# Making the sums of up-projection weight blocks during the input projection instead of in the first feed-forward block

## The chip, the cores and the metric

The kernel runs on one core of one Trainium2 chip. A core has a matmul engine (TensorE, PE in the profile, with its weight loads as PEld), a vector engine (VectorE, DVE), an activation engine (ScalarE, ACT), a general engine (GpSimd, POOL) and a queue engine (SyncE, SP) that only issues transfers. ACT and POOL issue transfers too. The metric is the device time of one execution, in microseconds (us); lower is better.

## The reference

One layer of a hybrid encoder is computed for two groups of requests that share the weights: one prompt of 2048 rows (16 tiles of 128) and 8 short sequences of 16 rows (one tile, the sample).

```python
def layer(x, ...):
    h = rms_norm(x, norm_g[0])
    z = h @ w_in                      # 1024 -> 3592: q, k, v of 8 attention heads; q, k, v, o and gates of 4 mLSTM heads
    att = rms_norm(band_attention(qa, ka, va, rel_table), g_att)   # own chunk of 64 and 8 chunks before
    hb = mlstm_sequence(qh, kh, vh, ig, lf, c0, n0, m0)            # matrix memory, running maximum
    x = x + rms_norm(concat([att, gated(hb)]) @ w_out, norm_g[1])
    x = x + rms_norm(conv_ffn(rms_norm(x, norm_g[2]), ...), norm_g[3])

def conv_ffn(h, buf, w_up, w_conv, b_conv, w_down):
    u = h @ w_up                      # 1024 -> 2 x 2816
    y = b_conv + sum(ext[:, j:j + S] * w_conv[j] for j in range(3))   # causal depthwise convolution
    gate, up = jnp.split(y, 2, axis=-1)
    return (gelu(gate) * up) @ w_down
```

What the change touches is `h @ w_up`, and there only when and where some sums of weight blocks are made.

## The kernel before

All products are made in a split form: each operand is divided into a rounded high part and the rest, and `mm3` (L103) issues three matmuls, high by high, high by low and low by high (L105, L106, L107 in the profile). The division of an operand is one ACT copy and one VectorE subtraction (`split`, L1323; the rows of L1324 and L1325).

The program has three parts.

**The input projection** (the loop at L1260). The 3592 columns are cut into 14 groups, and the rows into two halves, so there are 28 turns (`seq`). In a turn `group_rows` or `group_T` multiplies one group's weights with the half's rows and yields after every 12 matmuls; each yield is one step of the loop at L1288. In each step the next group's weights are loaded and divided bit by bit (`load_group`), and `pump` (L184) advances two software pipelines beside the projection: attention (`att_stream`, for the sample `attention_sample`) and the mLSTM (`mem_stream`), as long as a running account of estimated VectorE time stays behind a share of estimated TensorE time. Loads go through SP, stores of the projection through ACT.

**The output projection** (`project`, L970). Beside it `folds` (L1172) forms combinations of blocks of `w_down` in six spare tiles of 128 x 512 (`spare_tile`, L70): loads and stores on POOL's queue, subtractions on VectorE (L1184), each pinned behind what was written before it on its engine by `keep_in_program_order`. At its end `h2_units` builds the seven combinations B of the feed-forward input for the first block; four of them pass through DRAM (`lated`) and are divided later (`late_B`, L1163).

**The feed-forward network** (the loop at L1478) runs over three blocks of rows. The up-projection uses a seven-product scheme on 2 x 2 blocks: for each of 22 feature tiles the four stored blocks a11, a12, a22, a21 of `w_up` (128 x 512 each) and four sums of them

- s1 = a21 + a22, s2 = s1 - a11, s3 = a11 - a21, s4 = a12 - s2

give the weights of seven products: a11, s2, s3, s1 in the first group of a feature tile and a12, a22, s4 in the second. `load_quads` (L1329) brings them in, `load_up` (L1356) divides them. In the first block (`b == 0`) `load_quads` loads the four stored blocks through SP, makes the four sums on VectorE (L1341), stores them through POOL to a DRAM tensor `wsd` (L1343), and keeps three tiles for the second group. In the second and third block the sums are read from `wsd` through SP (L1352), seven loads for each feature tile. All these tiles come from a pool of eleven (`quad`, L1063).

A program that plans ahead orders each engine's instructions by a model of their durations; only pinned ones keep their written place behind the instruction before them. [...] A tile of a pool is written again only when those who read it before have signalled.

Of the kernel before, what the change touches and what calls it, by code (L numbers as in the profile page):

```python
# [13 lines left out]
ALU = mybir.AluOpType  # L14
# [14 lines left out]
NF = 22  # L29
# [21 lines left out]
def hymba_step(ctx: ExitStack, tc: tile.TileContext, I: dict, O: dict):  # L51
    nc = tc.nc
# [17 lines left out]
    def spare_tile(name):  # L70
        return spare.tile([P, 512], F32, tag="k", name=name)

    def dt_(shape, name):
        return dram.tile(shape, F32, tag=name, name=name)
# [52 lines left out]
    wsd = [dt_([P, 2048], f"wsd{f}") for f in range(NF)]  # L127
# [143 lines left out]
    def group_rows(wh, wl, half, chunks, dst, name, width=256, out=None):  # L271
        for ci, tiles in enumerate(HALVES[half]):
            for j, t in enumerate(tiles):
                ch = chunks[ci]
                acc = ps_mm(f"{name}_{t}")
                for k in range(KT):
                    w = slice(k * width, (k + 1) * width)
                    tt = slice(j * P, (j + 1) * P)
                    mm3(acc[:, :width], ch[:, 0, k, tt], ch[:, 1, k, tt], wh[:, w], wl[:, w],
                        start=(k == 0), stop=(k == KT - 1))  # L280
                    if k % 4 == 3:
                        yield 1.3, 0.0
                stage = pa.tile([P, 384], F32, tag="st", name=f"{name}_st{t}", bufs=2)
                evac_scaled(stage[:, :256], acc[:, :256], None)
                if width > 256:
                    nc.vector.tensor_copy(gates[:, gate_ix(t), :], acc[:, 256:width])
                s = 4 if t == SAMPLE else t // 4
                nc.scalar.dma_start(dst[s][:, 0 if s == 4 else t % 4, :], stage[:, :256])
                if out is not None and s >= 3:
                    nc.scalar.dma_start(out[s - 3][:, 0 if s == 4 else t % 4, :], stage[:, :256])  # L290
# [4 lines left out]
    def raw_tile(name):  # L295
        return pa.tile([P, LS], F32, tag="raw", name=name, bufs=3)
# [3 lines left out]
    def load_bias():  # L300
        rel.append(raw_tile("reln")[:HA, :SQ - 383])
        tc.keep_in_program_order(nc.sync.dma_start(rel[0], I["rel_rev"][:, 0:SQ - 383]))
# [528 lines left out]
    def prep(units):  # L831
        yield units
        yield FLUSH
# [229 lines left out]
    def quad(name):  # L1063
        return ffn.p3.tile([P, 512], F32, tag="q", name=name, bufs=11)
# [107 lines left out]
    def folds():  # L1172
# [17 lines left out]
        for k in range(NK + 1):  # L1190
# [19 lines left out]
            make(k, 1, 2, 1, sub)  # L1210
            yield

    GROUPS = ["va0", "qk0", "qk1", "va1", "qk2", "qk3", "qb0", "vo0", "qb1", "vo1", "qb2", "vo2", "qb3", "vo3"]
    SRC = {g: i for i, g in enumerate(["va0", "qk0", "qk1", "va1", "qk2", "qk3",
                                       "qb0", "vo0", "qb1", "vo1", "qb2", "vo2", "qb3", "vo3"])}

    def load_group(gi):

        i = SRC[GROUPS[gi]]
        src, n = (I["w_in0"], 2112) if i == 0 else (I["w_in1"][i - 1], 2048)  # L1220
        h = wpool.tile([P, 2112], F32R, tag="wh", name=f"wi{i}_h{gi}", bufs=2)
        l = wpool.tile([P, 2112], F32R, tag="wl", name=f"wi{i}_l{gi}", bufs=2)

        def steps():
            q = n // 2
            for s in range(2):
                raw = pr.tile([P, 1056], F32, tag="wraw", name=f"wi{i}_raw{s}")
                nc.sync.dma_start(raw[:, :q], src[:, s * q:(s + 1) * q])
                yield 0.0, 0.0
                yield 0.0, 0.0  # L1230
                for e in range(2):
                    c = slice(s * q + e * q // 2, s * q + (e + 1) * q // 2)
                    r = raw[:, e * q // 2:(e + 1) * q // 2]
                    nc.scalar.copy(h[:, c], r)
                    nc.vector.tensor_tensor(l[:, c], r, h[:, c], op=ALU.subtract)
                    yield 0.0, 0.6

        return h, l, steps()
# [18 lines left out]
        pass  # L1257
    next(norms)
    load_bias()
    for n_, (half, gi) in enumerate(seq):  # L1260
        wh, wl, _ = pend
        split = iter([])
        if n_ + 1 < len(seq):
            pend = load_group(seq[n_ + 1][1])
            split = pend[2]
        g = GROUPS[gi]
        i = int(g[2])
        nm = f"{g}_{half}"
        if g[:2] == "va":
            it = group_rows(wh, wl, half, chunks, vd[i], nm, 264 if gi == 0 else 256,  # L1270
                            [O["v_prompt"][i], O["v_sample"][i].unsqueeze(1)])
        elif g[:2] == "qk":
            it = group_T(wh, wl, half, chunks, [qTd[i], kTd[i]], [-(DA ** -0.5), None], nm,
                         [None, [O["k_prompt"][i], O["k_sample"][i]]])
        elif g[:2] == "qb":
            it = group_T(wh, wl, half, chunks, [[t_[:, c, :] for t_ in qkbd[i]] for c in range(2)],
                         [None, DH ** -0.5], nm)
        else:
            it = group_rows(wh, wl, half, chunks, vobd[i], nm)
        if half == 0 and gi == 13:  # L1280
            chunks = []
            norms = norm_steps(1)
        if n_ == len(seq) - 1:
            out = project([0, 1, 2, 3, 4, 5, 6, 7, SAMPLE, 8, 9, 10, 11, 12, 13, 14, 15])
            split = w_out_steps()
            next(split)
            next(out)
        for u, (pe, dve) in enumerate(it):  # L1288
            ahead = []
            if n_ < len(seq) - 1 or u >= 6:  # L1290
                ahead.append(next(split, (0.0, 0.0)))
            if n_ == len(seq) - 1 and u == 12:
                ahead.append(next(out))
            if (half == 0 and gi == 13 and u >= 6 and u % 2 == 0) or (gi == 0 and u % 2 == 0):
                ahead.append(next(norms, (0.0, 0.0)))
            pump(pe + sum(a[0] for a in ahead), dve + sum(a[1] for a in ahead))
        for _ in split:
            pass
        if gi == 0:
            if half == 0:  # L1300
                nc.sync.dma_start(bgate, I["b_gate"].broadcast_to([P, 8]))
                nc.sync.dma_start(gatt, I["g_att"])
                heads.append(build_bias)
                mems.append(lambda: prep(prep_sample()))
            mems.append(lambda half=half: prep(prep_prompt(half)))
        if g[:2] == "qk":
            attention(i, half)
            if half == 0 and i == 3:
                heads.insert(len(heads) % 4, lambda: attention_sample(0, EARLY))
            if half == 1 and i == 0:  # L1310
                heads.insert(len(heads) % 4, lambda: attention_sample(EARLY, DB))
        if g[:2] == "vo":
            mems.append(lambda i=i, half=half: mlstm(i, half))
            if half == 0:
                mems.append(lambda i=i: mlstm_sample(i))
    for cost in out:
        pump(*cost)
    nc.sync.dma_start(O["m_prompt"], mrow[:, 16, :])
# [5 lines left out]
        nc.scalar.copy(h, r)  # L1324
        nc.vector.tensor_tensor(l, r, h, op=ALU.subtract)  # L1325

    raws = {}

    def load_quads(b, f, g):  # L1329

        src = lambda i: I["w_up"][f][:, i * 512:(i + 1) * 512]
        if b == 0 and g == 0:
            q = []
            for i in range(4):
                q.append(quad(f"wu{f}_{i}"))
                nc.sync.dma_start(q[i], src(i))
            a11, a12, a22, a21 = q
            s1, s2, s3, s4 = [quad(f"ws{f}_{i}") for i in range(4)]
            for o, x, y, op in ((s1, a21, a22, ALU.add), (s2, s1, a11, ALU.subtract), (s3, a11, a21, ALU.subtract),
                                (s4, a12, s2, ALU.subtract)):  # L1340
                nc.vector.tensor_tensor(o, x, y, op=op)  # L1341
            for i, o in enumerate((s2, s3, s1, s4)):
                nc.gpsimd.dma_start(wsd[f][:, i * 512:(i + 1) * 512], o)  # L1343
            raws[f] = [a12, a22, s4]
            return [a11, s2, s3, s1]
        if b == 0:
            return raws.pop(f)
        kept = lambda i: wsd[f][:, i * 512:(i + 1) * 512]
        out = []
        for i, s_ in enumerate([[src(0), kept(0), kept(1), kept(2)], [src(1), src(2), kept(3)]][g]):  # L1350
            r = quad(f"wu{b}_{f}_{g}_{i}")
            nc.sync.dma_start(r, s_)  # L1352
            out.append(r)
        return out
# [123 lines left out]
    for b, tiles in enumerate(FBLOCKS):  # L1478
# [48 lines left out]
        g, parts = {}, {}  # L1527
# [155 lines left out]
        if fast:  # L1683
# [96 lines left out]
            for p, (_, _, set_, onto) in enumerate(SEQUENCE):  # L1780
                for c in range(3):
# [19 lines left out]
                    for k in range(4 * c, min(4 * c + 4, NK)):  # L1801
                        i = 6 * p + k // 2
# [193 lines left out]
```

## Time and profile before

| | us |
|---|---|
| median of 3 runs | 2758.59 |
| lowest and highest run | 2757.4, 2761.65 |
| the profiled execution: its own time | 2761.56 |
| the profiled execution: its span | 2759.8 |

The granted clock of TensorE over the profiled execution is 0.988 of full speed. In the trace the input projection reaches to about 1022 us, the output projection from 1023 to 1327 us, the first block's up-projection from 1327 to 1668 us and its down-projection to about 1840 us; the second block follows to about 2330 us and the third to the end.

A row of grouped instructions reads: line, engine, operation, output <- inputs, count, then durations in ns. A row of waits reads: the engine and line that waited, whom it waited for, us in total, how many times, the longest. A row of a stage reads: from:to and its length, then the busy time of PE, PEld, DVE, ACT and POOL with counts of instructions, the granted clock, the share of the 16 DMA engines and GB/s. In order of time a row begins with its start and its duration, and ends in brackets with the idle time of the engine before it and what ended it.

### The profile page before, as it was taken

Reading aid. Unit: us, or ns where it says so; the run is one execution under the profiler, and the core shown is the slowest. Engines: PE = TensorE matmul, PEld = TensorE weight load, DVE = VectorE, ACT = ScalarE, POOL = GpSimd, SP = SyncE. Lnnn points to the kernel's source line nnn. Section 1 sums busy time; section 2 is a strip of 40 time slices with the busy share of each in tenths; the row PEclk is TensorE's granted clock in tenths of the full one; section 3 lists DMA queues with packets and bytes.
Section 4 is the critical chain, followed back from the end, with each engine's and each line's share of the span. In section 5 each row is a group of like instructions: output and inputs, shape, how many; then the busy total and the mean of one; then the engine's idle time right before and its main releaser. Section 6 shows DMA issues by size and latency. Waiting matters only on the chain.

```text
span 2759.8 us, 47655 instructions
## 1 busy us (share of the span) xinstructions
PE 2659.9 (96%) x16459; PEld 2481.2 (90%) x16459; DVE 1862.4 (67%) x3536; ACT 1417.6 (51%) x2887; POOL 700.7 (25%) x1325
## 2 busy tenths in 40 slices
PE   8899999999999999979899999999999999999998
PEld 7899999999799998867799998889999878999976
DVE  5345445644355666556898998758888776899956
ACT  4345544533355665433454456655454665555554
POOL 1100000211000002344655542023333212466401
PEclk9999999999999999989999999999999999999999
DMA  5634454556743554469877768766786777788775
GB/s 173 171 114 138 122 186 140 172 176 196 225 135 116 157 178 146 146 228 308 298 246 215 214 198 265 251 208 195 223 219 192 228 252 238 213 246 237 253 257 183
DMA packets 333711, 555.70 MB, mean 201 GB/s; under 512 B 61762, under 2 KB 169374, under 8 KB 333150
## 3 DMA queue, kind: packets, MB, share of 16 engines
q1 hardware_dynamic: 250798, 405.03, 47.5%
q0 software_dynamic: 44080, 113.81, 14.1%
q10 hardware_dynamic: 38592, 33.83, 3.7%
q8 instruction: 129, 2.11, 0.3%
q14 instruction: 112, 0.92, 0.1%
HBM read 389.77 MB, written 172.18 MB: 204 GB/s over the span
## 4 chain that ended last, share of the span: by engine, by line
PE 41%; DMA 5%; DVE 4%; issue 2%; ACT 1%; POOL 0%; DVEq 0%; SPq 0%; POOLq 0%; ACTq 0%
PE uec L105 5%; PE uec L106 5%; PE uec L107 5%; PE dn L107 3%; PE dn L105 3%; PE dn L106 3%; PE ua L107 3%; PE ua L106 3%; PE ua L105 3%; DMA wu<-in_w_up 2%; PE dnm L107 1%; PE dnm L106 1%; PE dnm L105 1%; PE ub L107 1%; PE ub L106 1%
## 5 line engine op out<-in xcount | busy, mean ns | idle before, releaser
L105 PE MATMUL uec<-B,wuh 128*128 128x384 f32 (+1 forms) x720 | 236.6, 329 | 9.2 <-DVE ug L1495 5.9
L106 PE MATMUL uec<-B,wuh 128*128 128x384 f32 (+1 forms) x720 | 235.4, 327 | 0.0
L107 PE MATMUL uec<-B,wul 128*128 128x384 f32 (+1 forms) x720 | 234.3, 327 | 0.0
L1324 ACT CAST wuh<-wu 128x512 fp32r<-128x512 f32 x255 | 141.6, 618 | 102.6 <-PE uec L106 98.7
L107 PE MATMUL dn<-wdh,al 128*128 128x512 f32 x462 | 186.0, 403 | 3.4 <-DVE al L1325 3.4
L105 PE MATMUL dn<-wdh,ah 128*128 128x512 f32 x462 | 183.6, 397 | 5.9 <-ACT ah L1324 4.0
L1325 DVE TENSOR_TENSOR al<-ar,ah 128x768 fp32r<-128x768 f32 (+2 forms) x141 | 108.4, 779 | 118.4 <-ACT ah L1324 114.8
L106 PE MATMUL dn<-wdl,ah 128*128 128x512 f32 x462 | 182.8, 396 | 0.0
L1324 ACT CAST ah<-ar 128x768 fp32r<-128x768 f32 (+2 forms) x141 | 96.2, 692 | 153.2 <-PE dnm L106 113.9
L1325 DVE TENSOR_TENSOR wul<-wu,wuh 128x512 fp32r<-128x512 f32 x255 | 164.3, 682 | 2.4 <-ACT wuh L1324 2.4
L663 POOL TENSOR_SCALAR ad<-ad 128x2 f32<-128x2 f32 x32 | 6.3, 195 | 615.3 <-DVE ad L661 615.3
L410 DVE CUSTOM_DVE_ANT_0 tmp<-s,nb 128x640 f32<-128x640 f32 (+4 forms) x128 | 94.1, 737 | 100.1 <-PE s L400 99.5
L105 PE MATMUL vo<-wi_h,hT 128*128 128x256 f32 x544 | 155.5, 286 | 0.0
L107 PE MATMUL vo<-wi_h,hT 128*128 128x256 f32 x544 | 155.3, 285 | 0.0
L106 PE MATMUL vo<-wi_l,hT 128*128 128x256 f32 x544 | 154.9, 285 | 0.0
L1325 DVE TENSOR_TENSOR wdl<-wdr,wdh 128x512 fp32r<-128x512 f32 x231 | 145.3, 684 | 8.2 <-ACT wdh L1324 8.0
L105 PEld LDWEIGHTS uec<-B,wuh 128*128 128x128 f32 x720 | 135.2, 188 | 13.6 <-issue 6.8
L105 PE MATMUL qk<-hT,wi_h 128*128 128x384 f32 (+1 forms) x384 | 130.3, 339 | 9.9 <-ACT qk_st L239 6.2
L411 ACT ACTIVATE tmp<-tmp,mn 128x640 f32<-128x640 f32 (+4 forms) x128 | 97.7, 763 | 77.0 <-DVE mn L410 72.6
L106 PEld LDWEIGHTS uec<-B,wuh 128*128 128x128 f32 x720 | 135.4, 188 | 0.2
L107 PEld LDWEIGHTS uec<-B,wul 128*128 128x128 f32 x720 | 135.1, 188 | 0.0
L1324 ACT CAST wdh<-wdr 128x512 fp32r<-128x512 f32 x231 | 127.4, 619 | 11.8 <-PE uec L106 7.4
(473 smaller groups left out, 9101.8 us busy)
## 6 DMA issues: line engine op xcount, KB each, us to landing
wu<-in_w_up SPq DMA_DIRECT2D x220, 256.0 KB, 4.8
wu<-wsd SPq DMA_DIRECT2D x176, 256.0 KB, 4.7
wdr<-wtd SPq DMA_DIRECT2D x132, 256.0 KB, 5.1
wi_raw<-in_w_in SPq DMA_DIRECT2D x52, 512.0 KB, 4.2
wdr<-in_w_down SPq DMA_DIRECT2D x99, 256.0 KB, 4.7
wsd<-ws POOLq DMA_DIRECT2D x88, 256.0 KB, 4.8
ar<-ad_S SPq DMA_DIRECT2D x50, 384.0 KB, 4.0
kraw<-kTd SPq DMA_DIRECT2D x112, 128.0 KB, 3.1
```

What stands on the lines that cost most here:

```text
L105: nc.tensor.matmul(out, ah, bh, start=start, stop=False, skip_group_check=onto)
L106: nc.tensor.matmul(out, ah, bl, start=False, stop=False, skip_group_check=onto)
L107: nc.tensor.matmul(out, al, bh, start=False, stop=stop, skip_group_check=onto)
L410: nc.vector.tensor_tensor_reduce(o_, s_, b_, 1.0, 3e38, ALU.add, ALU.min, accum_out=mn)
L411: nc.scalar.activation(tmp[:, :n], tmp[:, :n], AF.Exp, bias=mn, scale=-1.0, accum_out=rsum[:, i % 4, hh:hh + 1])
L663: nc.gpsimd.tensor_scalar(ad, ad, 1.0 / DH, 0.0, op0=ALU.mult, op1=ALU.add)
L1324: nc.scalar.copy(h, r)
L1325: nc.vector.tensor_tensor(l, r, h, op=ALU.subtract)
```

## The change

The sums are made by a new generator, `up_sums`, in the six spare tiles. It is advanced once in every step of the input projection from the third turn on (`n_ >= 2`), and whatever is left of it is run before the output projection's loop. For each feature tile it loads the four stored blocks through SP (two, a step, two), passes eight steps, makes the four sums on VectorE in four steps (three of them in place: s3 over a21, s2 over a11, s4 over a12), and stores them through POOL to `wsd` in two steps. Loads, sums and stores are pinned. `load_quads` loses its special case: the first block reads its seven weights as the two others do. The scheme's sums and the layout of `wsd` are as before. The short description of the change also speaks of sample attention in four column positions and of masks in DRAM; the kernel before has both, and the diff does not touch them.

```diff
+    def up_sums():
+
+        keep = tc.keep_in_program_order
+        for f in range(NF):
+            a11, a12, a22, a21 = q = [spare_tile(f"up{f}_{i}") for i in range(4)]
+            for i in range(4):
+                keep(nc.sync.dma_start(q[i], I["w_up"][f][:, i * 512:(i + 1) * 512]))
+                if i == 1:
+                    yield
+            for _ in range(8):
+                yield
+            s1 = spare_tile(f"up{f}_s")
+            for o, x, y, op in ((s1, a21, a22, ALU.add), (a21, a11, a21, ALU.subtract), (a11, s1, a11, ALU.subtract),
+                                (a12, a12, a11, ALU.subtract)):
+                keep(nc.vector.tensor_tensor(o, x, y, op=op))
+                yield
+            for i, o in enumerate((a11, a21, s1, a12)):
+                keep(nc.gpsimd.dma_start(wsd[f][:, i * 512:(i + 1) * 512], o))
+                if i % 2:
+                    yield
+
...
     load_bias()
+    sums = up_sums()
     for n_, (half, gi) in enumerate(seq):
...
         for u, (pe, dve) in enumerate(it):
             ahead = []
+            if n_ >= 2:
+                next(sums, None)
...
+    for _ in sums:
+        pass
     for cost in out:
         pump(*cost)
...
-    raws = {}
-
     def load_quads(b, f, g):
 
         src = lambda i: I["w_up"][f][:, i * 512:(i + 1) * 512]
-        if b == 0 and g == 0:
-            q = []
-            for i in range(4):
-                q.append(quad(f"wu{f}_{i}"))
-                nc.sync.dma_start(q[i], src(i))
-            a11, a12, a22, a21 = q
-            s1, s2, s3, s4 = [quad(f"ws{f}_{i}") for i in range(4)]
-            for o, x, y, op in ((s1, a21, a22, ALU.add), (s2, s1, a11, ALU.subtract), (s3, a11, a21, ALU.subtract),
-                                (s4, a12, s2, ALU.subtract)):
-                nc.vector.tensor_tensor(o, x, y, op=op)
-            for i, o in enumerate((s2, s3, s1, s4)):
-                nc.gpsimd.dma_start(wsd[f][:, i * 512:(i + 1) * 512], o)
-            raws[f] = [a12, a22, s4]
-            return [a11, s2, s3, s1]
-        if b == 0:
-            return raws.pop(f)
         kept = lambda i: wsd[f][:, i * 512:(i + 1) * 512]
```

## The prediction

> **What bounds the kernel now.** I read the page first, then busy time by stage, then who waited for whom in the stages that the diff touches.
>
> ```profile
> span 2759.8 us, 47655 instructions
> PE 2659.9 (96%) x16459; PEld 2481.2 (90%) x16459; DVE 1862.4 (67%) x3536; ACT 1417.6 (51%) x2887; POOL 700.7 (25%) x1325
> ```
>
> TensorE sets the end: it is busy for 2659.9 of 2759.8 us, so an edit can save at most the time in which TensorE idles or runs below its pace. Three stages by busy time: the stretch of the input projection in which the new sums would run, the up-projection of the first feed-forward block, and that of the second.
>
> ```profile
> core 0: us, PE busy (x) PEld busy (x) DVE busy (x) ACT busy (x) POOL busy (x), PEclk, DMA share, GB/s
> 80.00:928.00 848.00, 825.52 (x6267) 801.12 (x6266) 405.54 (x1014) 406.46 (x990) 52.86 (x160) 0.99 0.52 156
> 1326.70:1666.00 339.30, 326.97 (x1827) 318.92 (x1826) 315.99 (x488) 169.04 (x268) 182.40 (x271) 0.99 0.73 229
> 1843.00:2165.00 322.00, 321.47 (x1837) 319.96 (x1836) 266.92 (x402) 162.51 (x268) 105.03 (x197) 1.00 0.72 203
> ```
>
> The second block does the same matmuls (1837 records against 1827) in 322.0 us where the first takes 339.3. What differs is VectorE: 316.0 of 339.3 us (93%) against 266.9 of 322.0 (83%). TensorE's waits in the first block, from 1326 to 1672 us, and then all of them in the second:
>
> ```profile
> PE uec L105 <- DVE ug L1495: 5.9, 3, 3.7
> PE ua L107 <- DVE wul L1325: 2.0, 2, 1.6
> PE ua L105 <- ACT wuh L1324: 1.0, 2, 0.7
> ...
> PE dn L105 <- ACT wdh L1324: 0.5, 1, 0.5
> ```
>
> The first block waits for VectorE; the second has a single wait. The longest one, looked up on VectorE in order of time:
>
> ```profile
> 1494.57 0.69 DVE L1341 TENSOR_TENSOR ws<-wu,wu 128x512 f32<-128x512 f32 x1 [5.14 <-DMA wu<-in_w_up]
> 1495.18 1.01 DVE L1515 SCALAR_TENSOR_TENSOR y<-uu,wcv,y 128x768 f32<-128x768 f32 x1
> 1496.11 0.68 DVE L1341 TENSOR_TENSOR ws<-ws,wu 128x512 f32<-128x512 f32 x1
> 1496.71 0.55 DVE L1495 TENSOR_TENSOR ug<-x,uec 128x384 f32<-128x384 f32 x1
> ```
>
> A sum of two freshly loaded blocks stood at the head of VectorE and waited 5.14 us for its load, and the evacuation `ug` behind it, for which TensorE waited, came late. The diff takes this out of the block.
>
> **The change part by part.** *Removed from block 0.* The sums and their stores:
>
> ```profile
> L1341 DVE TENSOR_TENSOR ws<-wu,wu x44: 672/683/694, 1311.4 to 1640.4; 128x512 f32<-128x512 f32 x44
>   DMA wu<-in_w_up: 17.1, 9
> L1343 POOL DMA_DIRECT2D wsd<-ws x88: 539/539/1740, 1312.3 to 1642.0; - x88
> DMA to landing us min/median/max: 2.3/4.8/8.9
> ```
>
> The four sums of a feature tile, 88 in all at 0.683 us, are 60.1 us of VectorE, with 17.1 us of waits before them. Without the 60.1, VectorE has some 256 us of work in block 0, less than the 267 with which the second block runs unhindered. On the queues, 88 stores (four of 256 KB per feature tile) leave POOL and 66 more loads (seven instead of four) go onto SP: 22 x 256 KB less to move. The new loads are those that the second block makes already, so its 322.0 us is my estimate of block 0's floor: a gain of 17.3 us at most. Not all of it: the late B parts are still split at its start, behind the end of the output projection. I take **-15** (bounds -6, if only the first two wait rows, 7.9 us, go and 2 come back, and -18).
>
> Part of this is the clock. Three slices around the longest wait:
>
> ```profile
> 1460.00:1480.00 20.00, 20.00 (x117) 20.00 (x116) 19.48 (x31) 11.50 (x19) 7.82 (x11) 1.00 0.53 176
> 1480.00:1500.00 20.00, 15.45 (x81) 14.34 (x81) 14.86 (x26) 8.76 (x15) 10.85 (x19) 0.91 0.79 247
> 1500.00:1520.00 20.00, 20.00 (x108) 20.00 (x107) 16.78 (x27) 7.77 (x13) 9.02 (x16) 0.92 0.70 195
> ```
>
> In the last two TensorE started 189 matmuls, 45 fewer than two slices at 117: 7.7 us at 0.171 us each, of which 4.55 are idle and 3.1 the lowered clock. The Trainium skill ("TensorE: Matmul & The Clock Gate", part 1) says that TensorE falls to half clock after an idle window of about 3.4 us and needs as long to come back; the 3.7 us wait and the 0.91 agree. By that rule the four shorter waits of block 0 cost no clock and -15 stands; by it too a new stall in the projection costs its own length and about 3 us more only where it exceeds the window.
>
> *End of the output projection.* The first feature tile's sums stand here too:
>
> ```profile
> 1311.35 0.69 DVE L1341 TENSOR_TENSOR ws<-wu,wu 128x512 f32<-128x512 f32 x1 [3.49 <-DMA wu<-in_w_up]
> ...
> 1313.29 1.22 DVE L212 TENSOR_TENSOR mt<-mT_pt,mt 128x1024 fp32r<-128x1024 f32 x1
> 1314.56 0.51 PE L107 MATMUL wo<-wo,mt 128*128 128x512 f32 x1 [4.24 <-DVE mt L212]
> ```
>
> The subtraction `mt`, for which TensorE idled 4.24 us, stood behind a sum that waited 3.49 us for its load. That goes, but the splits of the same blocks wait for the same loads and can take its place: bounds 0 and -4, I take **-2**.
>
> *Added to the input projection.* Per feature tile four loads on SP, four sums on VectorE, four stores on POOL, over 15 steps of the group loop; 22 x 15 = 330 steps out of the 366 that groups 2 to 27 offer, so the tiles are free again before the folds of the output projection want them. A step's length:
>
> ```profile
> L105 PE MATMUL qk<-hT,wi_h x384: 277/336/688, 48.7 to 721.7; 128*128 128x384 f32 x160, 128*128 128x256 f32 x32
> L107 PE MATMUL vo<-wi_h,hT x544: 276/281/367, 258.2 to 1021.9; 128*128 128x256 f32 x182
> ```
>
> Groups 1 to 27 have 378 steps in 1021.9 - 48.7 = 973 us, 2.57 us each; a feature tile takes 38.6 us and the sums end near 930 us. VectorE rises from 405.5 to 466 us in the 848, 55%. That lies beside matmuls: a neighbouring stretch carried more without any loss.
>
> ```profile
> 900.00:1000.00 100.00, 100.00 (x801) 99.92 (x800) 64.46 (x162) 64.85 (x167) 7.19 (x21) 1.00 0.53 153
> ```
>
> If that cover were gone, one sum on the path costs 0.68 us, all of them 60. The transfers add 176 x 256 KB = 46 MB. Block 0 moves 229 GB/s at a share of 0.73, so 46 MB are about 147 us of all engines, and the share rises from 0.52 to 0.69, below the 0.72 of the second block. Landings get longer, but few of TensorE's waits here are for a transfer. The larger rows from 80 to 928 us:
>
> ```profile
> PE qk L105 <- ACT qk_st L239: 6.2, 1, 6.2
> PE ss L874 <- DMA sk6kh<-in_cache_k: 3.2, 1, 3.2
> PE qk L105 <- ACT qk_st L237: 3.1, 1, 3.1
> PE pt L77 <- ACT tmp L411: 2.6, 1, 2.6
> ```
>
> The exposed places are the start (the bias is still being written) and the sample attention near 713 us, which waits for its cache loads. POOL has 52.9 us of work in 848, and 88 issues of 0.54 add 48; VectorE waits for its small powers at the end of a head, up to two issues (1.1 us) longer. No row shows the price for TensorE: bounds 0 and +25 (below, first rival); I take **+4**, a quarter of these four rows' 15.1 us, nearer the free end because of the 900 to 1000 us row.
>
> *Sum:* -15 - 2 + 4 = **-13 us**. The profiled execution took 2761.6 us (span 2759.8), 3 above the median of 2758.6; against the median that is 2746.
>
> **The rivals.** *SP's queue is held (slower).* Each set of loads takes over tiles whose stores went out two steps, 5.1 us, before. A store is issued up to 1.1 us late and lands after 4.8, at worst 8.9: SP stands 0.8 us in the middle case, up to 4.9, at each of 21 boundaries, and behind it stand the loads of attention heads, weights and caches. Passed on whole to TensorE that is 17 to 103 us; it decides from 17 us on, where nothing of the gain is left. A fifth gives +21 in place of +4: 2763. Against it stands how much waiting on SP the projection bears already:
>
> ```profile
> SPq L1228 <- DVE wi_l L1235: 52.6, 21, 9.0
> SPq L368 <- DVE kl L364: 45.1, 16, 8.2
> SPq L354 <- DVE attT L442: 38.1, 7, 8.4
> SPq L1228 <- DMA wi_raw<-in_w_in: 34.1, 13, 4.6
> ```
>
> These four rows alone hold SP for 170 us, and TensorE idles 22.5 us in the whole stretch. The Trainium skill ("DMA: Bandwidth & Descriptors", anatomy of one DMA) states that a semaphore wait is served on the issuing sequencer before dispatch, so what is queued behind a waiting load waits too; these rows agree, and it says nothing of how much reaches TensorE. Chance 0.12.
>
> *The sums wait at the head of VectorE in the new place.* The folds of the output projection work with the same tiles and pinned order:
>
> ```profile
> DVE fold L1184 <- DMA fold<-in_w_down: 19.2, 7, 7.3
> ```
>
> 37 folds waited 19.2 us there, 0.52 each; 88 sums at that rate are 46 us of VectorE. A quarter on TensorE's path is +11 and the end 2753. Against it: a fold follows its load by two or three steps, these sums by nine, 23 us, and the worst landing above is 8.9. Chance 0.13.
>
> *Block 0 is not bound by the sums alone.* Seven loads per feature tile through a saturated start give only the -6, no gain before it, +4 in the projection: 2757. Against it: the second block with the same loads has one wait. Chance 0.15.
>
> *The projection takes it all for nothing:* -17 - 4: 2737. Chance 0.10.
>
> **How the numbers follow.** Forecast 2746, chance 0.50, its own range 2740 to 2752. The range runs from 2736 to 2759: it leaves out the first rival and a little below the last. A measurement here tells about 0.2% (5.5 us) from no change, so faster means below 2753.1. Faster: 0.49 of the forecast, 0.10, half of the VectorE rival (0.06), 0.03 of the block-0 rival: 0.68. Same: 0.01, 0.06, 0.11 and 0.02 of the first: 0.20. Slower: the rest, 0.12.
>
> **What would show it.** Right: the block-0 up-projection takes 322 to 326 us with VectorE near 260 and under 3 us of waits on TensorE; from 80 to about 930 us the projection is at most 8 us longer, VectorE 60 us busier, and TensorE's new waits are single ones. Wrong: SP rows in which later loads stand behind a store of sums, with TensorE waiting for those loads; VectorE rows in which a sum waits for `w_up`; or a block 0 that still takes over 332 us.

## The result and the profile after

The changed kernel takes 2791.4 us (median of 4 runs, 2785.1 to 2796.9) against 2760.1 us (4 runs) for the kernel before on the same chip: a ratio of 1.011, 95% interval 1.008 to 1.0137. It is about 30 us slower; 13 us faster was forecast. The profiled execution took 2791.1 us. The top of its page:

```profile
span 2789.4 us, 48030 instructions
PE 2673.4 (96%) x16459; PEld 2485.2 (89%) x16459; DVE 1868.1 (67%) x3536; ACT 1414.6 (51%) x2887; POOL 675.4 (24%) x1325
```

TensorE is busy for 13.6 us more with the same matmuls (its granted clock is 0.986 against 0.988, which is some 5 of 2670 us, so the clock alone is not all of it), and idle for 16 us more. Busy time by stage, cut at the last matmul `vo` (end of the input projection), the last `wo` (end of the output projection) and the first `dn` of L107 (end of the first block's up-projection); first before, then after. What follows takes 1091.2 us before and 1091.0 after:

```profile
80.00:921.90 841.90, 819.42 (x6215) 795.02 (x6214) 401.23 (x1004) 401.27 (x975) 52.86 (x160) 0.99 0.52 157
921.90:1021.90 100.00, 98.10 (x769) 97.42 (x769) 65.65 (x162) 65.57 (x166) 7.59 (x22) 0.98 0.55 162
1021.90:1326.70 304.80, 276.07 (x1418) 229.01 (x1417) 183.14 (x361) 133.49 (x335) 110.96 (x213) 0.95 0.66 215
1326.70:1668.60 341.90, 329.57 (x1842) 321.39 (x1840) 318.46 (x492) 171.39 (x272) 182.89 (x271) 0.99 0.73 228
```

```profile
80.00:932.90 852.90, 813.81 (x6056) 779.85 (x6057) 424.05 (x1026) 379.67 (x926) 95.22 (x233) 0.99 0.63 197
932.90:1032.90 100.00, 99.04 (x790) 98.49 (x788) 67.06 (x157) 61.67 (x152) 13.18 (x29) 1.00 0.67 200
1032.90:1371.50 338.60, 303.07 (x1567) 250.30 (x1565) 211.64 (x433) 157.35 (x398) 113.39 (x219) 0.93 0.66 212
1371.50:1698.40 326.90, 322.34 (x1837) 319.50 (x1836) 270.92 (x402) 170.79 (x272) 105.69 (x190) 1.00 0.74 223
```

The first block's up-projection is 15.0 us shorter (341.9 to 326.9), VectorE there at 270.9 us: the forecast gain is there in these two executions (below, how far such a stage varies). The input projection ends 11 us later (1032.9 against 1021.9); from 80 us to 100 us before its end, the first row of each view, TensorE idles 39.1 us (852.9 - 813.8) where it idled 22.5 (841.9 - 819.4). And the output projection takes **33.8 us longer** (338.6 against 304.8), a stage to which the change adds little. Its row shows more work: 1567 matmul records where there were 1418. Two groups of TensorE's instructions in that stage, scores of attention and memory of the mLSTM, before and after:

```profile
L399 PE MATMUL s<-kh,qs 128*128 128x320 f32 x28 | 9.7, 355 | 0.9 <-DVE ptl L423 0.9
...
L715 PE MATMUL ma<-cst,mqk 128*128 128x129 f32 x38 | 7.8, 289 | 0.0
```

```profile
L399 PE MATMUL s<-kh,qs 128*128 128x320 f32 x42 | 14.0, 341 | 0.0
...
L715 PE MATMUL ma<-cst,mqk 128*128 128x129 f32 x48 | 10.7, 306 | 5.1 <-DVE w L709 2.4 <-DVE attT L442 1.4 <-DVE cst L718 1.1
```

Of the 149 more, 99 belong to attention and 46 to the mLSTM: work that was done beside the input projection before and is left over now. (Up to its end the input projection has 143 matmul records fewer, 7279 against 7422.) So most of the loss arises in the input projection and shows a stage later. Towards the end of the output projection both kernels run thin, the changed one more and with a lower clock for longer; 1200 to 1300 us, before and after:

```profile
1200.00:1250.00 50.00, 40.00 (x174) 31.93 (x173) 29.93 (x48) 18.68 (x40) 26.05 (x46) 0.83 0.79 272
1250.00:1300.00 50.00, 44.53 (x206) 34.95 (x205) 32.91 (x46) 18.61 (x40) 25.49 (x51) 0.97 0.88 290
```

```profile
1200.00:1250.00 50.00, 35.73 (x175) 28.82 (x174) 25.61 (x72) 19.25 (x64) 16.52 (x35) 0.82 0.63 196
1250.00:1300.00 50.00, 44.04 (x187) 34.92 (x186) 28.75 (x47) 17.20 (x37) 27.34 (x46) 0.84 0.73 255
```

What held the new instructions, in the waits of the changed kernel from 80 to 1036 us, and then one row of the sums, by line:

```profile
DVE up_s L1227 <- DMA up<-in_w_up: 22.9, 5, 12.8
SPq L1219 <- DMA wsd<-up: 14.6, 12, 3.6
POOL wsd L1230 <- DVE up L1227: 380.3, 20, 60.4
```

```profile
L1227 DVE TENSOR_TENSOR up<-up,up x44: 672/684/894, 117.6 to 1089.0; 128x512 f32<-128x512 f32 x44
```

All three kinds of holding that one could fear are in this trace: sums waiting for loads on VectorE, loads waiting for stores on SP, and, longest, stores waiting for sums on POOL, with the mLSTM's POOL work behind them. The sums run until 1089 us, not 930. So there were three theories. **A: held queues**, the three waits above. **B: volume**, that is 60 us of VectorE and 46 MB of transfers, which delay every step of attention and mLSTM. **C: the plan**, which before the run puts attention and mLSTM later in TensorE's order.

### The profile page after: what moved, and what is told of

It is laid out like the page before. It is cut to its first block, busy times and chain, and to the rows that moved or that the text cites. A ratio compares the mean times of both kernels' runs of the same rounds, so it can differ in the third digit from the quotient of the medians.

```text
span 2789.4 us, 48030 instructions
## 1 busy us (share of the span) xinstructions
PE 2673.4 (96%) x16459; PEld 2485.2 (89%) x16459; DVE 1868.1 (67%) x3536; ACT 1414.6 (51%) x2887; POOL 675.4 (24%) x1325
## 4 chain that ended last, share of the span: by engine, by line
PE 47%; DMA 3%; DVE 2%; issue 1%; POOL 0%; ACT 0%; SPq 0%; DVEq 0%; POOLq 0%; ACTq 0%
PE uec L105 6%; PE uec L106 6%; PE uec L107 6%; PE dn L107 4%; PE dn L105 3%; PE dn L106 3%; PE ua L107 3%; PE ua L105 3%; PE ua L106 3%; PE ub L105 2%; PE ub L106 1%; PE dnm L107 1%; PE ub L107 1%; PE dnm L106 1%; PE dnm L105 1%
## 5 line engine op out<-in xcount | busy, mean ns | idle before, releaser
L107 PE MATMUL uec<-B,wul 128*128 128x384 f32 (+1 forms) x720 | 234.4, 327 | 0.0
L1350 ACT CAST wuh<-wu 128x512 fp32r<-128x512 f32 x315 | 172.8, 618 | 86.9 <-PE uec L106 83.6
L1351 DVE TENSOR_TENSOR wul<-wu,wuh 128x512 fp32r<-128x512 f32 x315 | 202.2, 683 | 2.8 <-ACT wuh L1350 2.4
L107 PE MATMUL dn<-wdh,al 128*128 128x512 f32 x462 | 186.1, 403 | 4.0 <-DVE al L1351 3.7
L107 PE MATMUL vo<-wi_h,hT 128*128 128x256 f32 x544 | 154.8, 285 | 0.0
L107 PEld LDWEIGHTS uec<-B,wul 128*128 128x128 f32 x720 | 135.1, 188 | 0.0
L423 DVE TENSOR_TENSOR ptl<-pt,pth 128x640 fp32r<-128x640 f32 (+4 forms) x128 | 93.5, 737 | 56.5 <-ACT pth L422 55.6
```

The costliest lines, as they stand in the source:

```text
L107: nc.tensor.matmul(out, al, bh, start=False, stop=stop, skip_group_check=onto)
L423: nc.vector.tensor_tensor(s.ptl[:, sl, qc], ptv, s.pth[:, sl, qc], op=ALU.subtract)
```

## The experiments

Most of them leave block 0 as it was and add the work in the input projection as a dummy, into a scratch tensor that nobody reads; what they cost is then the price of the added work alone. A summary, stages in us from one profiled execution each, ratio to the kernel before over all runs:

| run | median | ratio (95%) | input proj. | output proj. | block 0 up |
|---|---|---|---|---|---|
| before | 2752.5 to 2760.1 | | 1021.9 | 304.8 | 341.9 |
| after | 2791.4 | 1.0109 (1.008 to 1.0137) | 1032.9 | 338.6 | 326.9 |
| d_all | 2816.8 | 1.0204 (1.0178 to 1.0231) | 1038.6 | 348.8 | 338.2 |
| d_load | 2777.7 | 1.008 (1.0049 to 1.011) | 1046.1 | 314.7 | 338.2 |
| d_sum | 2774.9 | 1.006 (1.0038 to 1.0082) | 1029.6 | 317.0 | 340.6 |
| d_store | 2770.4 | 1.0038 (1.0019 to 1.0057) | 1032.0 | 307.9 | 335.3 |
| d_tiny | 2762.9 | 1.0011 (0.9999 to 1.0023) | 1027.0 | 309.3 | 332.1 |
| a_free | 2797.4 | 1.0148 (1.0124 to 1.0173) | 1078.4 | 299.3 | 326.9 |
| d_quiet | 2776.4 | 1.0064 (1.0039 to 1.0089) | 1037.2 | 304.0 | 340.2 |
| d_busy | 2785.3 | 1.0095 (1.0077 to 1.0113) | 1020.2 | 336.4 | 337.8 |
| d_load_pool | 2783.6 | 1.0105 (1.0081 to 1.013) | 1029.8 | 319.7 | 333.9 |
| b_order | 2742.3 | 0.9961 (0.9949 to 0.9974) | 1020.9 | 295.7 | 333.3 |
| b_pool | 2782.3 | 1.011 (1.0092 to 1.0128) | 1017.8 | 303.1 | 368.0 |
| a_pin | 2780.2 | 1.0096 (1.0067 to 1.0126) | 1060.4 | 299.9 | 329.7 |

The kernel before had a median of 2760.1, 2758.3, 2758.2, 2752.5 and 2754.8 us beside the changed kernel and in the four groups of runs below. Stage times of a single execution differ by some us between kernels that do the same there (block 0 is the same in the kernel before and in the eight dummies and takes 332.1 to 341.9, 337.6 in the mean), so nothing smaller than that is read from them.

### All of the work as a dummy, and each part alone

```diff
+    wsx = [dt_([P, 2048], f"wsx{f}") for f in range(NF)]
+    def up_dummy():
...
+                keep(nc.gpsimd.dma_start(wsx[f][:, i * 512:(i + 1) * 512], o))
...
+    sums = up_dummy()
...
+            if n_ >= 2:
+                next(sums, None)
```

The generator is otherwise `up_sums`, and `load_quads` is that of the kernel before.

> The kernel before, with the changed kernel's loads, sums and stores made beside it in the input projection; the sums go to a scratch tensor that nobody reads, and block 0 makes its own sums as before. Theory A (the loads, sums and stores hold one another on their queues, each waiting for the last): the whole loss of the change stands here without block 0's gain, so +45 us (13 + 32 of the projection stages), 2805. Theory B (the additional work itself: 60 us of VectorE, 46 MB): also +45. Theory C (the plan fixed before the run places attention and mLSTM later): also about +45, and attention's matmuls fall behind the projection's as in the changed kernel. If it is under +20, the loss belongs to something that the change does with block 0's loads.

> The same without sums and stores: 88 loads of 256 KB through SP into the spare tiles, at the same steps. Theory A: a load waits here for nothing but the load before it in the same tile, which landed long ago; within 5 us of the kernel before. Theory B: 23 MB, half the transfers; +5 to +15. Theory C: 88 pinned instructions on SP; +5 to +15 with the attention behind the projection in the order of TensorE.

> The same with the sums alone, on five spare tiles that are filled with zeros once: 88 VectorE instructions of 0.68 us, no loads, no stores. Theory A: no wait, so within 5 us. Theory B: 60 us of VectorE on top of 55% use; if VectorE's work is what costs, +20 or more. Theory C: the plan has to make room for 60 us of VectorE at pinned places; +10 to +30, with attention behind.

> The same with the stores alone: 88 stores of 256 KB on POOL's queue out of tiles of zeros that are never written again. Theory A: they wait for nothing, and POOL only issues them (48 us); within 5 us. Theory B: 23 MB and 48 us of POOL; +5 to +15. Theory C: 88 pinned instructions on POOL; +5 to +15. If loads, sums and stores alone come to under 15 us together and all of them to 45, the loss lies in the waits between them.

In `d_load` only the loads stand in the generator; in `d_sum` only the sums, over five tiles that are zeroed once (their values are not used); in `d_store` only the stores out of such tiles. The steps between them are kept.

Measured: all together 1.0204, 56 us at 2758 us. After's loss is 30, and the 15 us that block 0 gives back make it 45, as expected; 11 us of `d_all` are left. By stages, `d_all` is longer than the changed kernel by 5.7 us in the input projection, 10.2 in the output projection (where its first sums of block 0 still stand) and 11.3 in block 0; why the first two are not nought was not tested. Alone, the loads cost 22 us, the sums 16.5, the stores 10.5: 49 us of the 56. No part alone has a wait of one kind for another (SP stands some 15 us behind its own earlier loads in `d_load`, POOL 11 us behind its own earlier stores in `d_store`), so theory A, which wanted each within 5 us, explains at most the remaining 7. Theory B had the stores within its range; the loads cost more than its +15, the sums a little less than its +20 (both intervals reach into the range). Theory C had the sums and the stores within its ranges, so these runs do not part it from B. Of the 60 us of VectorE 16.5 us reach the end, although VectorE was busy for under half of that stretch (405.5 of 848 us). The 23 MB of stores, for which nobody waits, add 10.5 us while the mean DMA share rises from 0.52 to 0.57:

```profile
80.00:932.00 852.00, 817.49 (x6165) 790.94 (x6166) 397.04 (x984) 396.88 (x964) 91.51 (x229) 0.99 0.57 177
```

Do the stores delay other transfers? Two of the larger groups, by the time from issue to landing, from 80 to 930 us (line, count, KB each, median us), before and then with the stores alone:

```profile
kraw<-kTd SPq DMA_DIRECT2D x92, 128.0 KB, 3.2
vobd<-vo_st ACTq DMA_DIRECT2D x57, 128.0 KB, 2.4
```

```profile
kraw<-kTd SPq DMA_DIRECT2D x88, 128.0 KB, 3.7
vobd<-vo_st ACTq DMA_DIRECT2D x55, 128.0 KB, 3.5
```

Attention and mLSTM read q, k and v back from DRAM, so such differences could make their steps begin later. That this is the path of the 10.5 us is not shown: of the 20 groups with 12 or more transfers 13 land later and 6 earlier with the stores alone, but 13 land later and 7 earlier also in `d_tiny` (next section), which costs next to nothing.

### The same instructions without their volume; the pins taken off

Against `d_all`, for `d_tiny`:

```diff
-                keep(nc.sync.dma_start(q[i], I["w_up"][f][:, i * 512:(i + 1) * 512]))
+                keep(nc.sync.dma_start(q[i][:, :8], I["w_up"][f][:, i * 512:i * 512 + 8]))
```

The sums and stores of `d_tiny` are cut to the same eight columns, so 63/64 of each sum is left out. In the changed kernel (`a_free`):

```diff
-        keep = tc.keep_in_program_order
+        keep = lambda ins: ins
```

> The kernel before with all of the added instructions beside an unchanged block 0, at the same steps, pinned alike, but each over 128x8 columns instead of 128x512, so 1/64 of the volume. If the pinned instructions' number and places cost (they bind the order of three engines), nearly all of the +58 us stays: over +40. If their volume costs (60 us of VectorE, 46 MB), almost nothing stays: under +8. Between these, both.

> The changed kernel with the pins taken off: loads, sums and stores may be planned anywhere. If the pins cost, most of the +31 us goes: 2760 to 2768, or below 2758 where the whole of block 0's 15 us is left. If the volume costs: 2780 to 2800, as before. If what counts is that a sum meets a load that isn't there, it is slower, since a free sum can be planned right behind its load: over 2800.

Measured: `d_tiny` costs 1.0011 (0.9999 to 1.0023), an interval that reaches no change. The 264 pinned instructions, their number, their places and the waits among them are nearly free. Its waits on POOL, VectorE and SP:

```profile
POOL wsx L1233 <- DVE up L1230: 423.8, 25, 61.8
DVE up_s L1230 <- DMA up<-in_w_up: 19.7, 4, 8.6
SPq L1222 <- DMA wsx<-up: 21.2, 9, 4.8
```

POOL stood 423.8 us behind waiting stores (440 in the changed kernel, in two rows of 380.3 and 59.6), VectorE 19.7 us behind waiting loads (22.9), and SP 21.2 us behind waiting stores (14.6): the same holding, and no loss that can be told from none. This takes theory A out for all three. (POOL, with little to do, waits in the kernel before too: 595.2 us from 80 to 1036 us for the mLSTM's `ad`.) Where 63/64 of the volume goes, the loss goes: it is the volume that costs. Whether it costs while the program runs or through the plan, which reckons with the shorter instructions too, this run does not settle.

Without pins the loss is no smaller (1.0148, 1.0124 to 1.0173); the input projection then ends at 1078 us. But this run changes more than the pins: the plan now makes all sums between 17 and 331 us, in place of 111 to 1089. TensorE falls behind there, at a DMA share of 0.89; the kernel before, then `a_free`:

```profile
80.00:331.00 251.00, 241.72 (x1645) 239.44 (x1644) 111.05 (x247) 120.29 (x276) 3.40 (x8) 0.97 0.43 130
```

```profile
80.00:331.00 251.00, 220.74 (x1404) 212.28 (x1404) 136.48 (x306) 97.62 (x224) 44.03 (x83) 0.96 0.89 261
```

So it says that the same work costs in another place too, not what the pins alone are worth.

### Where in the projection it costs

Against `d_all`:

```diff
-            if n_ >= 2:
+            if 2 <= n_ <= 10 or 20 <= n_ <= 24:
                 next(sums, None)
...
-        for f in range(NF):
+        for f in range(11):
```

This is `d_quiet`; in `d_busy` the condition is `11 <= n_ <= 19 or n_ >= 25`. Both make the sums of 11 feature tiles only.

> The kernel before with loads, sums and stores for 11 of the 22 feature tiles (into scratch, block 0 unchanged), at the full rate, only in turns 2 to 10 and 20 to 24 of the projection, in which mostly prompt attention runs beside it. If the cost is even, half of the +58 us of all: +25 to +32. If it stands in the stretch with mLSTM and sample attention (about 400 to 750 us and the end): under +12.

> The same 11 feature tiles only in turns 11 to 19 and from 25 on, in which the mLSTM and the sample attention run beside the projection. If the cost is even: +25 to +32, as the other half. If it stands in this stretch: over +40.

Measured: 1.0064 and 1.0095, 18 and 26 us for eleven feature tiles each, 44 together. The cost does not stand in one stretch alone: that would have been under 12 and over 40. Whether it is even is open: `d_busy` lies in the +25 to +32 of an even cost and `d_quiet` below it, but their intervals overlap, and an even 22 each would lie in both. What differs clearly is where the loss lands. In the quiet turns it lengthens the input projection by 15 us and leaves the output projection alone; in the turns with mLSTM and sample attention the input projection ends on time, and the output projection takes 32 us longer, with 1555 matmul records, close to the changed kernel's 1567. The output projection of the one and of the other:

```profile
1037.20:1341.20 304.00, 275.74 (x1451) 231.18 (x1450) 186.98 (x375) 137.31 (x346) 113.30 (x213) 0.94 0.65 212
```

```profile
1020.20:1356.60 336.40, 298.58 (x1555) 249.17 (x1554) 211.30 (x431) 153.75 (x386) 117.19 (x234) 0.93 0.68 222
```

### Another queue for the loads

Against `d_load`:

```diff
-                keep(nc.sync.dma_start(q[i], I["w_up"][f][:, i * 512:(i + 1) * 512]))
+                keep(nc.gpsimd.dma_start(q[i], I["w_up"][f][:, i * 512:(i + 1) * 512]))
```

> The run with the 88 loads alone, with the loads issued on POOL's queue instead of SP's; the same 23 MB at the same steps. If a load costs because it takes a place in SP's order (attention, mLSTM and weight loads stand behind it), the +19 us go: under +6. If the transfers cost wherever they are issued (longer landings of everything else): +12 to +22, as the loads on SP and the stores on POOL did.

Measured: 1.0105, 29 us, over both expectations. Taking the loads out of SP's order gains nothing. The Trainium skill ("Trainium Kernel Development and Optimization", Key Constraints) says that transfers issued from different queues run on the same 16 engines, and that another issuer saves only issue time; this run agrees, its 29 us against 22. The run gives up a place in SP's order for one in POOL's, where POOL now stands 31.0 us, in 27 waits, behind earlier ones of these loads; by `d_tiny` such places and waits alone are nearly free. Whether POOL's queue is really dearer by some 7 us (the intervals overlap) was not tested.

### TensorE's order taken from the kernel before

```diff
+PE_ORDER = (
...
+def pin_pe(tc):
...
+    pe = [i for i in tc.nc.cur_bb.bb.instructions if i.engine == mybir.EngineType.PE]
...
+        tc.add_manual_dep(cur, prev.name, info, reason="pin_pe")
```

`PE_ORDER` holds the order that the plan gave the 15914 TensorE instructions in the kernel before, by their place in the program as written, which both kernels share. Each is tied behind the one before it, in issue order alone.

> The changed kernel with TensorE's order fixed to the one that the plan of the kernel before has (the same 15914 instructions of TensorE in both; each is tied behind the one that stood before it there); the other engines' orders are planned anew round it. If the loss is that the plan lets attention and mLSTM fall behind the projection, the order of before takes it away and block 0's gain shows: 2740 to 2755. If the loss is made at run time, because each step of attention and mLSTM is later by the sums and transfers between, TensorE waits for them in the old places instead: 2780 or more, with the output projection short again and the input projection longer by the whole loss.

Measured: 1.0096; the loss stays. The time of 2780.2 us and the stages are what was expected of a loss made at run time: the output projection is back at 299.9 us, and the input projection now ends at 1060.4, 38.5 us late. Theory C falls as far as TensorE's order goes: the plan only decides *in which stage* the loss shows. With the old order TensorE stands in the old places and waits. Three stretches of the kernel before, then of this run:

```profile
600.00:650.00 50.00, 49.82 (x404) 47.71 (x403) 22.79 (x80) 20.05 (x61) 8.51 (x28) 1.00 0.71 213
700.00:750.00 50.00, 45.18 (x408) 36.72 (x407) 12.60 (x32) 15.95 (x37) 1.26 (x4) 0.97 0.72 226
750.00:800.00 50.00, 46.83 (x377) 46.27 (x376) 28.11 (x55) 28.70 (x64) 0.00 (x0) 1.00 0.46 136
```

```profile
600.00:650.00 50.00, 40.59 (x284) 37.08 (x283) 24.59 (x76) 15.57 (x46) 12.13 (x33) 0.97 0.74 232
700.00:750.00 50.00, 44.75 (x395) 34.60 (x393) 15.91 (x53) 10.96 (x28) 5.48 (x16) 0.90 0.76 253
750.00:800.00 50.00, 41.12 (x330) 37.38 (x323) 21.81 (x42) 19.93 (x44) 3.75 (x7) 0.91 0.80 254
```

VectorE is busy for 24.6, 15.9 and 21.8 of 50 us there: far from full, while TensorE loses 9.2 us in the first stretch alone. The larger waits of TensorE from 80 to 1400 us say for whom:

```profile
PE cus L798 <- DMA cs<-in_state_c: 8.5, 6, 2.3
...
PE rt L77 <- DVE cm L571: 6.5, 1, 6.5
PE s L399 <- ACT kh L363: 6.3, 1, 6.3
PE pt L77 <- ACT tmp L411: 6.1, 4, 2.6
PE ss L874 <- DMA sk6kh<-in_cache_k: 5.2, 1, 5.2
PE ms L703 <- DVE w L709: 4.5, 4, 1.8
```

State and cache loads of the samples, evacuations and weights of attention and mLSTM: no single place, but steps of chains in which TensorE, ACT, VectorE and a transfer follow one another. Not held fixed in this run are the orders of the other engines, which were planned anew.

### What block 0's gain is made of

```diff
             for i in range(4):
                 q.append(quad(f"wu{f}_{i}"))
+            for i in (3, 2, 0, 1):
                 nc.sync.dma_start(q[i], src(i))
```

(`b_order`, in the kernel before) and, apart from it, `b_pool`, in the kernel before too:

```diff
-                nc.vector.tensor_tensor(o, x, y, op=op)
+                e = nc.gpsimd if o is s3 or o is s4 else nc.vector
+                e.tensor_tensor(o, x, y, op=op)
```

> The kernel before, the sums in block 0 as they were, only the four loads of a feature tile in the order in which the sums want them (a21, a22, a11, a12 in place of a11, a12, a22, a21). If block 0's 15 us are the sums' waits for their loads (17 us on VectorE), the first block gets 5 to 12 us shorter: 2746 to 2753. If they are VectorE's volume there (60 us), no change: 2756 to 2761.

> The kernel before with two of the four sums of a feature tile (s3, s4) made by POOL in block 0 instead of VectorE: 30 us of VectorE's volume leave block 0, and nothing is added to the projection. If VectorE's volume bounds block 0, the up-projection of the first block gets 6 to 10 us shorter: 2748 to 2752. If POOL's own work there (182 of 342 us, with copies that the convolution waits for) becomes the bound, no gain or slower: 2758 to 2775.

Measured: `b_order` takes 2742.3 us, **0.9961 (0.9949 to 0.9974)**: 10 us faster than the kernel before beside it (2752.5), within the 5 to 12 us of the first expectation, and so faster than the changed kernel too, whose ratio is 1.011. The first sum, s1 = a21 + a22, had wanted the third and fourth block loaded; now it wants the first two. Its rows of the sums and of the first block's up-projection:

```profile
L1342 DVE TENSOR_TENSOR ws<-wu,wu x44: 677/684/693, 1299.6 to 1619.2; 128x512 f32<-128x512 f32 x44
...
  DMA wu<-in_w_up: 3.7, 3
```

```profile
1316.60:1649.90 333.30, 327.09 (x1841) 322.03 (x1840) 317.24 (x490) 169.78 (x272) 182.21 (x274) 0.99 0.74 235
```

VectorE's waits for loads fall from 17.1 to 3.7 us. Its work in the block stays (317.2 us, 95% of the stage). Against the one execution of the kernel before the stage is 8.6 us shorter and the output projection 9.1, where TensorE's longest wait for `mt` at L212 went from 4.2 to 2.6 us. But 333.3 us lies within the 332.1 to 341.9 of the unchanged blocks, 4.3 below their mean, so the runs show the 10 us, and the traces do not show how they divide between the two stages.

`b_pool` is 30 us slower, beyond its worst expectation. One form of the sums that POOL makes, and VectorE's commonest instruction of block 0 before and in this run (1327 to 1668 us in both):

```profile
L1342 POOL TENSOR_TENSOR ws<-wu,wu x22: 1273/1316/2581, 1303.8 to 1657.5; 128x512 f32<-128x512 f32 x22
```

```profile
L1325 DVE TENSOR_TENSOR wul<-ws,wuh 128x512 fp32r<-128x512 f32 x60 | 39.7, 681 | 0.0
```

```profile
L1325 DVE TENSOR_TENSOR wul<-ws,wuh 128x512 fp32r<-128x512 f32 x56 | 51.7, 939 | 0.0
```

A sum of this form takes POOL 1.32 us in the median, one of the other form 1.73 (VectorE 0.68), and meanwhile this group of VectorE's two-input subtractions slows from 681 to 939 ns on average; the other three groups of that line go from about 681 to 835, 808 and 680. VectorE has 44 sums less to do in block 0 and is busier, 334.9 us against 318.5, and TensorE's six longest wait rows in the stage, 26.0 us together, all name VectorE:

```profile
1320.90:1688.90 368.00, 339.37 (x1841) 325.29 (x1840) 334.87 (x448) 170.02 (x272) 218.61 (x313) 0.98 0.69 212
```

The Trainium skill ("GPSIMD Engine Reference", 1. Specifications and 4.1 Engine selection) has both: POOL is about half as fast on two inputs, and it contends with VectorE's instructions that read two inputs. The rows agree.

## Why the prediction was wrong

**Block 0, -15: the direction was right, the size nearer 10, the reason open in part.** The stage shrank by 15.0 us between the two profiled executions, to 326.9 us, where 322 to 326 was forecast. But the nine traces with an unchanged block take 337.6 us in the mean and the three with the new one (after, `a_free`, `a_pin`) 327.8, so some 10 us are shown and the agreement with 15 is partly luck. VectorE was to be near 260 us and took 270.9: 318.5 fell by 47.6, not by 60.1. The rows that I quoted overlap (the first ends at 1495.26, the next begins at 1495.18), and busy time counts an overlap once, so the sums' durations could not simply be taken off. I had put the stage down to VectorE at 93% and counted the sums as the weight to be lifted. `b_order` lifts none of that weight and makes the whole kernel 10 us faster; the order of four loads was visible in the row that I quoted (the 5.14 us before a sum of `w_up` blocks) and read as an argument for moving the sums instead. How much of block 0's own gain is that order and how much the volume, the traces do not tell. (The wait rows that I showed of block 0 hold six shorter waits beside the one of 3.7 us, not four.)

**End of the output projection, -2:** not to be seen in the changed kernel, where the stage grew by 33.8 us. With the same wait shortened in `b_order` the stage was 9.1 us shorter in one execution, so the bound of -4 may have been too narrow; the wait itself is only 1.6 us shorter there.

**Input projection, +4 within 0 and +25: this step failed.** The added work costs 45 us in the changed kernel (30 and the 15 of block 0; some 40 by the mean of block 0) and 56 alone (`d_all`), over the upper bound. The step rested on two sentences. The first is that VectorE's 60 us lie "beside matmuls", because a neighbouring stretch carried more VectorE work (64%) without loss. `d_sum` shows 16.5 us for these 60. The 900 to 1000 us stretch shows that TensorE can be kept busy at that VectorE share, not that added work is free: what it delays can show later. The second is that only the waits of four of TensorE's rows in that stretch (15.1 us) can grow. TensorE's idle time there grew by 16.6 us (22.5 to 39.1), over four times the +4; and beside this the stage ended with 143 matmuls fewer done, which the output projection then had to do. In the sum the output projection's body had no term at all, and 33.8 us stand there. The transfers got the sentence that few of TensorE's waits are for a transfer; loads and stores alone cost 22 and 10.5 us. That the rows of the kernel before are short because the plan fills the waits of attention and mLSTM with projection matmuls is my reading; `a_pin`, where the old order makes TensorE wait in the input projection, fits it.

**The pace, 38.6 us for a feature tile and an end near 930 us:** the sums end at 1089 us. In `d_tiny` they end late too, at 1039 us, at nearly no cost, so a late end alone is not the cause.

**The rivals.** *SP's queue is held* named the right sign, and its row exists (14.6 us behind stores), but the loads alone cost 22 us where no store stands before them, no less on another queue, and `d_tiny` has 21.2 us of that wait at nearly no cost. *Sums at the head of VectorE*: the wait was 22.9 us, half of the 46 worked out, and 19.7 us of it in `d_tiny` do no harm. So two of the signs of being wrong that I had named were there and were not the cause. *Block 0 not bound by the sums alone*: its gain of 6 is too small for the 10 to 15 measured. *For nothing* did not come about. No rival had the added volume as its price; the 60 us that all sums would cost without cover, named under the change, were not given a chance.

**What stays open:** how the loss divides between a VectorE instruction standing in front of a chain's step and a transfer landing later. The three parts show that both kinds of work cost, but not through which step; and the 7 us by which the whole costs more than its parts lie within the runs' uncertainty. Nor is the share of the folds known: they use the same six tiles and begin 51 us behind the start of the output projection's stage (1084.0 us), where it was 30 before (1051.5). TensorE's wait rows of that stage name no fold.

## What to carry to other kernels

An engine's busy share of 48% did not tell the price of more work on it here, where dependent chains run through it: price moved work by putting it there as a dummy whose result nobody reads, before anything is taken away elsewhere, and look for the loss in the stage behind as well. Few waits on TensorE in a trace need not mean that delays are free: count also which side work is done by the end of the stage. And see how far a stage varies between kernels that do the same in it before its gain is explained. Before moving work away from an instruction that waits for its loads, load its operands first in the order in which it wants them: here that alone was worth 10 us.

## What the runs showed of the hardware

In `b_pool` POOL made a 128x512 sum in 1.32 or 1.73 us, by its form, and the largest group of VectorE's two-input instructions beside it took over a third longer (681 to 939 ns), other groups from nothing to 59% (`y` from `ug`, 1008 to 1601 ns); after giving POOL 30 us of its work VectorE was 16 us busier in the stage. And 23 MB of stores that nobody waits for cost 10.5 us of 2758 at a mean DMA share of 0.57.
